# Two down projections of an encoder block: from eight products of block halves to seven

## The chip, the cores and the metric

The kernel runs on one core of a Trainium2 chip. TensorE (PE in the profile, its weight loads PEld) multiplies, VectorE (DVE), ScalarE (ACT) and GpSimd (POOL) do everything else, and SyncE (SP) issues nearly all DMAs. The metric is the device time of one execution in microseconds, the median of three runs: 2277.6 us before (2276.05 to 2281.06).

## The reference, cut to what matters

One layer: a SwiGLU feed-forward network, a token mixer, a second feed-forward network, each inside the same frame of norms. All data are float32; 1024 tokens (S), width 1024 (D), hidden width 2816 (DFF).

```python
def swiglu(h, w_gu, w_down):
    g, u = jnp.split(h @ w_gu, 2, axis=-1)
    return (jax.nn.silu(g) * u) @ w_down
...
def sandwich(x, fn, g_pre, g_post, shift, scale, gate, res_w):
    h = modulate(rmsnorm(x, g_pre), shift, scale)
    y = rmsnorm(fn(h), g_post)
    return x + res_w * gate[:, None, :] * y
...
        mod = (c_act @ w_ada[l] + b_ada[l]).reshape(b, N_SUB, 3, D_MODEL)
...
        x = sandwich(x, ffn1, norm_pre[l, 0], norm_post[l, 0], mod[:, 0, 0], mod[:, 0, 1], mod[:, 0, 2], 0.5)
        x = sandwich(x, mix, norm_pre[l, 1], norm_post[l, 1], mod[:, 1, 0], mod[:, 1, 1], mod[:, 1, 2], 1.0)
        x = sandwich(x, ffn2, norm_pre[l, 2], norm_post[l, 2], mod[:, 2, 0], mod[:, 2, 1], mod[:, 2, 2], 0.5)
```

The change concerns the product with `w_down` (1024 x 2816 by 2816 x 1024), twice, and the nine vectors of `mod`.

## The kernel before

**Numbers.** Every float32 operand is split into a high and a low part (`split`, L135: a cast on ACT, a subtraction on DVE or POOL). A product is three matmuls: high by high, high by low, low by high. A matmul has a 128x128 stationary and a 128x512 moving operand.

**Stages.** First network: an up phase and a down phase; then the recurrent branch, its output (`rec_out_phase`), attention, the merge, the output projection; then the second network, up and down. In the networks PE, DVE, ACT and POOL run in the order in which the code issues (a manual schedule); SP's order, and all engines' order in `rec_out_phase`, come from the scheduler. Each engine works strictly in its order.

**Up phase.** 22 blocks of 128 hidden channels. The first 4 (second network: 3) are plain; the others (`block`, L614) use seven products of halves, Winograd's form of Strassen's scheme, in the order 1, 2, 6, 5, 7, 3, 4. After product i of block fb, `mix(fb + 1, i)` (L581) makes the next block's operand: up to two POOL operations, a cast on ACT, a subtraction on DVE. A block's activations (`act`, 128x1024) go to DRAM (`act_d`).

**Down phase** (L716 to L800). The 22 blocks of the inner dimension are loaded again in seven chunks (`CHUNKS`) of 2 to 4. `down_w` loads and splits one activation or weight block; for each chunk and each of 8 token blocks (`sb`) PE adds up the chunk's products in two PSUM banks, and DVE adds them to `yacc[sb]` (L779). This is the plain product: 22 x 8 x 2 x 3 = 1056 matmuls. The last two chunks are ordered by token halves, so that the first half's epilogue runs beside the second half's matmuls.

**Epilogue.** `put` does the row norm (a square on ACT, an addition and a power on POOL) and multiplies by the gate on POOL; `update` adds the residual on DVE, stores, and starts the next norm (`rstd_of`: ACT, then POOL twice); `norm` scales on DVE; `drain` lets PE transpose four normalized rows for the next stage. `push_last` (L407) ends the kernel.

**Background.** `bgq` is a queue of generators that compute the conditioning vectors; `bg(n)` advances it by n steps. A step of `ada_acc` (L179) loads 512 KB of `w_ada` and adds it to a sum on DVE; `ada_cols` (L193) and `ada_gate` (L259) end with a few matmuls on PE into banks of `trbank`. Before, five such vectors run in the first network (one step a block, one a row step of the down phase), two in `rec_out_phase` (three steps in each of eight iterations, then `bg_flush`).

**Tiles.** Tag `raw` has 3 tiles, `wh` and `wl` 4 each (operands high and low), `t4` 22 big ones, `u` 3. PSUM has 6 banks of tag `ps` and 2 of `tr`.

## Time and profile before

| | us |
|---|---|
| median of 3 runs | 2277.6 |
| profiled execution | 2280.03 |
| its span, first to last instruction | 2278.2 |
| PE busy in the span | 2212.8 |
| first down projection, from 488.0 | 263.2 |
| second down projection, from 2026.8 | 241.2 |

The page below gives the mean over whole slices of the span; the granted clock is nearly full throughout.

```profile
PEclk9999999999999999999999999999999999999999
GB/s 295 103 84 92 110 111 92 111 138 187 189 191 121 77 50 40 66 148 166 111 49 67 25 59 53 157 185 158 97 92 83 83 83 83 82 141 110 93 93 120
```

Each of the 40 columns is 57 us. The down phases are columns 9 to 13 and 36 to 40. Rows of groups read: line, engine, operation, output and inputs, shape, count, then busy time and the mean of one in ns, then the idle time before it and what ended it. The rows on which the argument rests stand with the prediction.

### The profile page before, as it was taken

How to read it: one execution, taken by the hardware profiler on the slowest of the kernel's cores; microseconds unless marked ns; L12 is line 12 of the kernel's file. 1: busy time of each engine (PE TensorE's matmuls, PEld its weight loads, DVE VectorE, ACT ScalarE, POOL GpSimd, SP SyncE). 2: the span in 40 equal slices, each digit the busy share in tenths (PEclk: the TensorE clock that was granted, in tenths of full speed). 3: DMA queues.
4: the chain of work that ended last, by engine and by line, in shares of the span. 5: the costliest groups of instructions: out<-in, count | busy, mean ns of one | idle time of the engine just before them, and what ended most of it. 6: DMA issues, size and time to landing. Idle time of an engine off the chain costs nothing.

```text
span 2278.2 us, 26296 instructions
## 1 busy us (share of the span) xinstructions
PE 2212.8 (97%) x10227; PEld 1837.7 (81%) x10227; DVE 1230.3 (54%) x1740; ACT 945.8 (42%) x1502; POOL 582.3 (26%) x412
## 2 busy tenths in 40 slices
PE   5999999999999999999999999999999999999998
PEld 3877888888778788888898988887788888888886
DVE  6665554535755677643336666546854444433444
ACT  3543333341213587821147777336433333342121
POOL 3432222222225311000021120006432222222224
PEclk9999999999999999999999999999999999999999
DMA  9322332345653211245312011454322222243223
GB/s 295 103 84 92 110 111 92 111 138 187 189 191 121 77 50 40 66 148 166 111 49 67 25 59 53 157 185 158 97 92 83 83 83 83 82 141 110 93 93 120
DMA packets 217748, 250.30 MB, mean 110 GB/s; under 512 B 10864, under 2 KB 172824, under 8 KB 217624
## 3 DMA queue, kind: packets, MB, share of 16 engines
q1 hardware_dynamic: 217512, 248.60, 34.4%
q8 instruction: 80, 1.31, 0.2%
q14 instruction: 44, 0.36, 0.1%
q10 hardware_dynamic: 112, 0.03, 0.0%
HBM read 203.51 MB, written 48.23 MB: 110 GB/s over the span
## 4 chain that ended last, share of the span: by engine, by line
PE 75%; DVE 6%; ACT 4%; DMA 2%; issue 1%; POOL 1%; DVEq 0%; POOLq 0%; ACTq 0%
PE pd L766 17%; PE pj L435 6%; PE pj L433 6%; PE pj L434 6%; PE psX L610 5%; PE psX L612 5%; PE psX L611 5%; PE pj L1064 4%; PE psZ L610 3%; PE psZ L612 3%; PE psZ L611 3%; PE pv L1111 1%; PE psY L610 1%; PE psY L612 1%; PE psY L611 1%
## 5 line engine op out<-in xcount | busy, mean ns | idle before, releaser
L766 PE MATMUL pd<-dh,ah 128*128 128x512 f32 x1440 | 348.9, 393 | 0.0
L766 PEld LDWEIGHTS pd<-dh,ah 128*128 128x128 f32 x1440 | 273.3, 190 | 57.5 <-POOL dh L137 0.5
L434 PE MATMUL pj<-hl,wh 128*128 128x512 f32 x576 | 227.6, 395 | 5.7 <-DVE hl L316 5.7
L435 PE MATMUL pj<-hh,wl 128*128 128x512 f32 x576 | 227.6, 395 | 4.7 <-DVE wl L137 4.1
L433 PE MATMUL pj<-hh,wh 128*128 128x512 f32 x576 | 230.1, 400 | 0.5 <-ACT wh L136 0.5
L779 DVE TENSOR_TENSOR yacc<-yacc,pd 128x512 f32<-128x512 f32 x190 | 121.9, 683 | 193.4 <-PE pd L766 193.2
L601 DVE TENSOR_TENSOR wm<-raw,wm 128x512 fp32r<-128x512 f32 x152 | 109.6, 724 | 160.5 <-ACT wm L600 160.5
L588 POOL TENSOR_TENSOR raw<-wsum,raw 128x512 f32<-128x512 f32 x37 | 48.1, 1299 | 365.7 <-DVE wm L601 360.4
L136 ACT CAST wh<-raw 128x1024 fp32r<-128x1024 f32 (+1 forms) x86 | 86.8, 1011 | 126.5 <-PE pj L434 52.6
L137 POOL TENSOR_TENSOR wl<-raw,wh 128x1024 fp32r<-128x1024 f32 x25 | 61.2, 2456 | 291.9 <-ACT wh L136 247.4
L434 PEld LDWEIGHTS pj<-hl,wh 128*128 128x128 f32 x576 | 109.8, 191 | 29.7 <-DVE hl L316 7.7
L435 PEld LDWEIGHTS pj<-hh,wl 128*128 128x128 f32 x576 | 109.7, 191 | 29.7 <-DVE wl L137 5.7
L433 PEld LDWEIGHTS pj<-hh,wh 128*128 128x128 f32 x576 | 109.8, 191 | 22.9 <-ACT wh L136 0.8
L137 DVE TENSOR_TENSOR wl<-raw,wh 128x1024 fp32r<-128x1024 f32 (+1 forms) x61 | 73.7, 1211 | 84.7 <-ACT wh L136 84.7
L610 PE MATMUL psX<-hh,wm 128*128 128x512 f32 x296 | 115.6, 391 | 2.8 <-ACT mixes L633 2.8
L610 PE MATMUL psX<-hs,wm 128*128 128x512 f32 x296 | 115.3, 389 | 1.6 <-ACT mixes L626 1.6
L612 PE MATMUL psX<-hh,wm 128*128 128x512 f32 x296 | 115.2, 389 | 0.0
L611 PE MATMUL psX<-hl,wm 128*128 128x512 f32 x296 | 115.2, 389 | 0.0
L612 PE MATMUL psX<-hs,wm 128*128 128x512 f32 x296 | 115.2, 389 | 0.0
L611 PE MATMUL psX<-hs,wm 128*128 128x512 f32 x296 | 115.2, 389 | 0.0
L136 ACT CAST dh<-rawd 128x1024 fp32r<-128x1024 f32 x54 | 56.4, 1052 | 138.8 <-DMA rawd<-in_ffn_w_down_dram 105.5
L1064 PE MATMUL pj<-hh,wh 128*128 128x512 f32 x256 | 102.3, 400 | 0.9 <-DVE gate L277 0.9
(303 smaller groups left out, 5283.9 us busy)
## 6 DMA issues: line engine op xcount, KB each, us to landing
rawa<-in_w_ada_dram SPq DMA_DIRECT2D x56, 512.0 KB, 4.3
raw<-in_ffn_w_gu_dram SPq DMA_DIRECT2D x49, 512.0 KB, 4.3
rawd<-act SPq DMA_DIRECT2D x44, 512.0 KB, 3.6
rawd<-in_ffn_w_down_dram SPq DMA_DIRECT2D x44, 512.0 KB, 4.0
raw<-in_w_in_dram SPq DMA_DIRECT2D x44, 512.0 KB, 3.8
sr<-in_ffn_w_gu_dram SPq DMA_DIRECT2D x39, 512.0 KB, 6.4
act<-act SPq DMA_DIRECT2D x37, 512.0 KB, 4.7
rawa<-in_w_ada_dram SPq DMA_DIRECT2D x32, 256.0 KB, 5.6
```

The costliest lines, as they stand in the source:

```text
L136: nc.scalar.copy(hi, raw)
L137: (eng or nc.vector).tensor_tensor(lo, raw, hi.bitcast(F32), op=ALU.subtract)
L433: nc.tensor.matmul(dst, wh[:, kk, :], xhk[:, sl], start=first, stop=False)
L434: nc.tensor.matmul(dst, wh[:, kk, :], xlk[:, sl], start=False, stop=False)
L435: nc.tensor.matmul(dst, wl[:, kk, :], xhk[:, sl], start=False, stop=last)
L601: nc.vector.tensor_tensor(t[:, 1], src, t[:, 0].bitcast(F32), op=ALU.subtract)
L610: nc.tensor.matmul(dst, t[:, 0, kk, :], xh, start=first and kk == 0, stop=False, skip_group_check=True)
L611: nc.tensor.matmul(dst, t[:, 0, kk, :], xl, start=False, stop=False, skip_group_check=True)
L612: nc.tensor.matmul(dst, t[:, 1, kk, :], xh, start=False, stop=last and kk == 3, skip_group_check=True)
L766: nc.tensor.matmul(pd[h], a_[:, tk], w_[:, h * 512 : (h + 1) * 512], start=(i == 0 and j == 0), stop=(i == n - 1 and j == 2),)
L779: nc.vector.tensor_tensor(yacc[sb][:, sl], yacc[sb][:, sl], pd[h], op=ALU.add)
L1064: nc.tensor.matmul(d, a[:, k, :], b[k][:, sl], start=k == 0 and i == 0, stop=k == KB - 1 and i == 2)
```

## The change

The down projection is computed in seven products in place of eight, with the same scheme as the up phase: tokens in two halves, output columns in two halves (`h1`, `h2`), and the inner dimension in 11 pairs of blocks (2j and 2j+1). The seven products run one after the other over all pairs; a *unit* (p, j) is pair j of product p: two loads of 256 KB into one `raw` tile (a half of an activation block, a half of a weight block), one split of 128x1024, and 4 x 3 = 12 matmuls.

- The sums of halves (four POOL operations a pair, for weights and for activations) are made during the up phase by `all_sums`, one step after each product of a block, and stored in DRAM (`act_s`, `down_s`). A pair is loaded one pair ahead. Activations of the Strassen blocks are summed in place, in the tiles that `block` left (`kept`), once both are done; those of plain blocks are loaded again.
- Products 1, 6, 7 and 4 add up in four banks (`chain`), the others in four more; between products ACT copies or DVE adds four banks to `yacc` (`reads`).
- Pairs 4 to 10 of product 4 are fetched between those of product 3 and kept in `t4` tiles. Product 4 then runs pairs 0 to 3 for all four rows of the second token half, and pairs 4 to 10 row by row; the first half's rows are complete with product 3.
- `push_last` reads the last bank directly, without adding it to `yacc` first.
- Background: a load is issued one step before its sum; a step that needs a bank can be held back; two steps a block in the up phase, one a unit in the down phase. Two vectors (`ada_cols(6)`, `ada_cols(7)`) move to `rec_out_phase`, which makes five steps an iteration.

```diff
+    raw_home = ["raw"]
+    BANK = "needs a bank"
     def ada_acc(v, alloc):
         acc = alloc("acc")
         for k in range(KB):
-            raw = wpool.tile([P, 1024], F32, tag="raw", bufs=3, name=nm("rawa"))
+            if raw_home[0] == "t4":
+                raw = t4("rawa")
+            else:
+                raw = wpool.tile([P, 1024], F32, tag="raw", bufs=3, name=nm("rawa"))
             nc.sync.dma_start(raw, w_ada[k * P : (k + 1) * P, v * D : (v + 1) * D])
+            yield None
             if k == 0:
                 nc.vector.tensor_scalar(acc, raw, c_act[:, 0:1], None, op0=ALU.mult)
             else:
                 nc.vector.scalar_tensor_tensor(
                     acc, raw, c_act[:, k : k + 1], acc, op0=ALU.mult, op1=ALU.add
                 )
-            yield None
+        yield None
         yield acc
...
+    at = [None]
+    def bg(n=1, banks=True):
         for _ in range(n):
-            while bgq:
+            while bgq and (banks or at[0] is not BANK):
                 try:
-                    next(bgq[0])
+                    at[0] = next(bgq[0])
                     break
                 except StopIteration:
+                    at[0] = None
                     bgq.pop(0)
...
-            for h, sl in enumerate(halves):
-                junk = tmp[0].tile([P, D], BF16, tag="junk", bufs=2, name=nm("junk"))
-                nc.vector.tensor_tensor(y[:, sl], y[:, sl], pd[h], op=ALU.add)
-                nc.scalar.activation(junk[:, sl], y[:, sl], AF.Square, scale=D ** -0.5, accum_out=sq[h])
-                if h == 0:
-                    nc.vector.tensor_tensor(y[:, sl], y[:, sl], g[:, sl], op=ALU.mult)
+            junk = [tmp[0].tile([P, D], BF16, tag="junk", bufs=2, name=nm("junk")) for _ in range(2)]
+            one = halves[1]
+            nc.scalar.activation(junk[1][:, one], y[:, one], AF.Square, scale=D ** -0.5, accum_out=sq[1])
+            nc.vector.tensor_tensor(y[:, one], y[:, one], g[:, one], op=ALU.mult)
             self.update(sb - 1)
+            one = halves[0]
+            nc.scalar.activation(junk[0][:, one], pd, AF.Square, scale=D ** -0.5, accum_out=sq[0])
+            nc.vector.tensor_tensor(y[:, one], pd, g[:, one], op=ALU.mult)
             r = small("rstd")
...
+            if fb % 2 == 0:
+                first_of[0] = act
+            elif fb - 1 >= direct:
+                kept[fb - 1, fb] = first_of[0], act
...
                     mix(fb + 1, i)
-                    if fb == NF - 1 and i in ORDER[3:]:
-                        down_w(0, ORDER[3:].index(i))
+                    next(jobs, None)
+                    if i in (2, 3):
+                        bg(1)
+                    if fb == NF - 1 and i in ORDER[4:]:
+                        units.fetch(ORDER[4:].index(i) + 1)
+                ready[0] = fb
                 block(fb, after)
...
+        PAIRS = NF // 2
+        STREAM = (1, 2, 6, 5, 7, 3, 4)
+        act_of = {1: (act_d, 0, 0), 2: (act_d, 1, 0), 4: (act_d, 1, 1), 6: (act_s, 0, 0),
+                  7: (act_s, 0, 1), 3: (act_s, 1, 0), 5: (act_s, 1, 1)}
+        down_of = {1: (w_down, 0, 0), 2: (w_down, 1, 0), 3: (w_down, 1, 1), 5: (down_s, 0, 0),
+                   7: (down_s, 0, 1), 4: (down_s, 1, 0), 6: (down_s, 1, 1)}
+        ready = [0]
...
+        kept = {}
+        def pair_load(j, weights):
+            if not weights and (2 * j, 2 * j + 1) in kept:
+                return kept.pop((2 * j, 2 * j + 1))
+            src = w_down if weights else act_d
+            top, bot = t4("top"), t4("bot")
+            nc.sync.dma_start(top, rows(src, 2 * j))
+            nc.sync.dma_start(bot, rows(src, 2 * j + 1))
+            return top, bot
+        def pair_sums(j, weights, top, bot):
+            dst = down_s if weights else act_s
+            t1, t2, b1, b2 = top[:, h1], top[:, h2], bot[:, h1], bot[:, h2]
+            add, sub_ = ALU.add, ALU.subtract
+            if weights:
+                steps = ((t1, t2, t1, sub_), (t2, b2, t2, sub_), (b2, b2, t1, sub_), (b1, b1, b2, sub_))
             else:
+                steps = ((b2, t2, b2, add), (t2, t1, t2, sub_), (t1, b2, t1, sub_), (b1, b1, t1, sub_))
+            for o, p, q, op in steps:
+                nc.gpsimd.tensor_tensor(o, p, q, op=op)
+                yield
+            yield
+            nc.sync.dma_start(rows(dst, 2 * j), top)
+            nc.sync.dma_start(rows(dst, 2 * j + 1), bot)
...
+            reload_ = [j for j in range(PAIRS) if 2 * j < direct]
+            todo = [(j, True) for j in range(PAIRS)]
+            for n, j in enumerate(reload_):
+                todo.insert(2 * n + 2, (j, False))
+            later = [j for j in range(PAIRS) if j not in reload_]
+            nxt = pair_load(*todo[0])
+            yield
+            yield
+            while todo or later:
+                if later and ready[0] > 2 * later[0] + 1:
+                    j = later.pop(0)
+                    yield from pair_sums(j, False, *pair_load(j, False))
+                elif todo:
+                    now, tiles = todo.pop(0), nxt
+                    if todo:
+                        nxt = pair_load(*todo[0])
+                    yield from pair_sums(*now, *tiles)
+                else:
+                    yield
+        jobs = all_sums()
...
+        class Units:
+            def __init__(self):
+                self.order = [(p, j) for p in STREAM for j in range(PAIRS)]
+                first, last = self.order[:-2 * PAIRS], self.order[-PAIRS:]
+                third = self.order[-2 * PAIRS : -PAIRS]
+                self.order = first
+                for j in range(PAIRS):
+                    self.order.append(third[j])
+                    if j + KEPT_FROM < PAIRS:
+                        self.order.append(last[j + KEPT_FROM])
+                self.order += last[:KEPT_FROM]
+                self.n, self.got = 0, {}
+            def fetch(self, n):
+                while self.n < min(n, len(self.order)):
+                    p, j = self.order[self.n]
+                    raw = wpool.tile([P, 2, 512], F32, tag="raw", bufs=3, name=nm("rawd"))
+                    for o, (t, k, half) in enumerate((act_of[p], down_of[p])):
+                        nc.sync.dma_start(raw[:, o], rows(t, 2 * j + k)[:, (h1, h2)[half]])
+                    if p == STREAM[-1] and j >= KEPT_FROM:
+                        hi, lo = t4("dh", F32R, (P, 2, 512)), t4("dl", F32R, (P, 2, 512))
+                    else:
+                        hi, lo = (wpool.tile([P, 2, 512], F32R, tag=t, bufs=4, name=nm("dh")) for t in ("wh", "wl"))
+                    split(raw, hi, lo, nc.gpsimd if p in (2, 5, 7) and j % 3 == 2 else nc.vector)
+                    self.got[p, j] = hi, lo
+                    self.n += 1
+            def take(self, p, j, ahead):
+                self.fetch(self.order.index((p, j)) + 1 + ahead)
+                return self.got.pop((p, j))
...
+            def mm(dst, i, ops, first, last):
+                hi, lo = ops
+                tk = slice(i * P, (i + 1) * P)
+                for n, (a_, w_) in enumerate(((hi, hi), (hi, lo), (lo, hi))):
+                    nc.tensor.matmul(
+                        dst, a_[:, 0, tk], w_[:, 1, :], start=first and n == 0, stop=last and n == 2,
+                        skip_group_check=True,
+                    )
...
+            reads = {
+                1: ((copy, 0, h1),), 2: ((add, 0, h1),), 6: ((copy, 0, h2),),
+                5: ((copy, half, h2), (add, 0, h2)), 7: ((add, half, h2),), 3: ((add, 0, h2),),
             }
...
+            chain = [bank("px"), bank("px"), trbank("px"), trbank("px")]
+            tr_home[0], raw_home[0] = "ps", "t4"
+            for p in STREAM[:-1]:
+                own = p in (1, 6, 7)
+                dst = chain if own else [bank("pv") for _ in range(4)]
+                for j in range(PAIRS):
+                    ops = units.take(p, j, 3)
+                    for i in range(half):
+                        mm(dst[i], i, ops, j == 0 and p not in (6, 7), j == PAIRS - 1)
+                    next(jobs, None)
+                    bg(1, own)
+                if p == 2:
+                    for _ in jobs:
+                        pass
+                if p == 7:
                     bg_flush()
...
+                for op, sb0, sl in reads[p]:
+                    for i in range(half):
+                        op(sb0 + i, sl, dst[i])
...
+            p = STREAM[-1]
+            for j in range(KEPT_FROM):
+                ops = units.take(p, j, 3)
+                for i in range(half):
+                    mm(chain[i], i, ops, False, False)
+                if j == 0:
+                    units.fetch(len(units.order))
+                epi.put(j, yacc[j])
+                if j > 0:
+                    epi.update(j - 1)
+                if j > 1:
+                    epi.norm(j - 2)
+            last_steps = {4: ((3,), (2, 3), 2), 5: ((4,), (), 4), 6: ((5,), (4,), 2), 7: ((6,), (5,), KB)}
+            for i in range(half):
+                sb = half + i
+                for j in range(KEPT_FROM, PAIRS):
+                    mm(chain[i], i, units.got[p, j], False, j == PAIRS - 1)
+                if tail and i == half - 1:
+                    epi.push_last(sb, yacc[sb], chain[i])
+                    break
+                copy(sb, h1, chain[i])
+                epi.put(sb, yacc[sb])
+                updates, norms, n_out = last_steps[sb]
+                for n in updates:
+                    epi.update(n)
+                for n in norms:
+                    epi.norm(n)
+                if ahead:
+                    ahead.fetch(i + 1)
+                    epi.drain(n_out, on_act=(1, 1))
+                epi.fetch(sb + 1)
...
-            bg(3)
+            bg(5)
...
-        bgq.extend([mixer_constants(), ada_cols(6), ada_cols(7), ada_gate(0, 0.5), ada_cols(3), ada_cols(4)])
+        bgq.extend([mixer_constants(), ada_gate(0, 0.5), ada_cols(3), ada_cols(4)])
...
-        bgq.extend([ada_gate(1, 1.0), ada_gate(2, 0.5)])
+        bgq.extend([ada_cols(6), ada_cols(7), ada_gate(1, 1.0), ada_gate(2, 0.5)])
```

106 lines of the change are left out of this document (27 added, 79 removed).

## The prediction

> **What bounds the kernel now.** I read the page's busy table first, then its chain, then the windows around the two down projections, then what TensorE waited for there.
>
> ```profile
> span 2278.2 us, 26296 instructions
> PE 2212.8 (97%) x10227; PEld 1837.7 (81%) x10227; DVE 1230.3 (54%) x1740; ACT 945.8 (42%) x1502; POOL 582.3 (26%) x412
> PE 75%; DVE 6%; ACT 4%; DMA 2%; issue 1%; POOL 1%; DVEq 0%; POOLq 0%; ACTq 0%
> 488.00:751.20 263.20, 257.32 (x1141) 212.29 (x1140) 153.39 (x165) 76.60 (x99) 86.21 (x53) 0.97 0.53 170
> 2027.00:2268.20 241.20, 239.69 (x1056) 197.67 (x1054) 99.00 (x123) 58.59 (x72) 78.33 (x42) 1.00 0.34 112
> 316.00:335.00 19.00, 19.00 (x86) 15.72 (x85) 9.75 (x14) 6.85 (x12) 5.57 (x4) 1.00 0.34 110
> PE pc L200 <- DVE acc L187: 3.8, 2, 2.2
> PE pd L766 <- POOL dl L137: 1.3, 1, 1.3
> ```
>
> PE is busy for 97% of the span, and three quarters of the chain is PE. In a window row come the length, then the busy time of PE, PEld, DVE, ACT and POOL, then the granted clock, the DMA share and GB/s. The second down projection (2027 to 2268.2) is 1056 matmuls in 239.69 us: **0.227 us a matmul**, with nothing between them. The first (488 to 751.2) has the same 1056 and lasts 263.2 us, because gate vectors (pc, pg) and transposes are done in between, PE waits for two of them (the 3.8 us), and the clock falls to 0.97. An up-projection block (316 to 335) leaves DVE half idle and POOL at 5.57 of 19 us. So a matmul taken away is time taken away, if the other engines then still feed PE.
>
> **The change, part by part.**
>
> *Matmuls.* A product has 11 pairs x 4 token blocks x 3 = 132; seven make 924 a projection in place of 1056. 2 x 132 x 0.227 = **-59.9**. The same shape is used (128x128 stationary, 512 moving), so I keep the rate.
>
> *Entry.* Each projection now begins with one 1.3 us wait for a POOL subtraction (the first is the last row above). The new first unit is split on DVE, and its load can start in the block before: **-2.7** for both; between -2.7 and +3, should the first load come late.
>
> *Gate vectors in the first projection.*
>
> ```profile
> 620.50:625.80 5.30, 3.12 (x17) 3.12 (x17) 3.32 (x3) 0.86 (x1) 1.05 (x1) 0.75 0.62 201
> 625.80:632.50 6.70, 6.70 (x22) 5.39 (x22) 0.80 (x3) 0.19 (x1) 0.00 (x0) 0.69 0.26 97
> ```
>
> Here PE waits for a DVE sum, does its 16 narrow matmuls, and then runs at clock 0.69: 22 matmuls in 6.7 us where 22 x 0.227 = 5.0 would do, so 1.7 are lost beside the wait. In the new order loads run a step ahead of their sums and the steps lie in the up phase. The matmuls stay; the waits (3.8) and twice the 1.7 may go: 7.2 at most, 0 at least. I take **-6**, nearer the rows.
>
> *Feeding the stream.* A unit is 12 matmuls, 12 x 0.227 = 2.72 us of PE.
>
> ```profile
> rawd<-act SPq DMA_DIRECT2D x44, 512.0 KB, 3.6
> raw<-in_w_att_o_dram SPq DMA_DIRECT2D x8, 256.0 KB, 2.9
> sr<-in_ffn_w_gu_dram SPq DMA_DIRECT2D x39, 512.0 KB, 6.4
> L136 ACT CAST dh<-rawd 128x1024 fp32r<-128x1024 f32 x54 | 56.4, 1052 | 138.8 <-DMA rawd<-in_ffn_w_down_dram 105.5 <-PE pd L766 19.8 <-DMA rawd<-act 13.5
> L137 DVE TENSOR_TENSOR dl<-rawd,dh 128x1024 fp32r<-128x1024 f32 x10 | 12.2, 1221 | 13.0 <-ACT dh L136 13.0
> L137 POOL TENSOR_TENSOR dl<-rawd,dh 128x1024 fp32r<-128x1024 f32 x22 | 57.9, 2633 | 173.3 <-ACT dh L136 172.0 <-PE pd L766 1.3
> L779 DVE TENSOR_TENSOR yacc<-yacc,pd 128x512 f32<-128x512 f32 x190 | 121.9, 683 | 193.4 <-PE pd L766 193.2
> ```
>
> A raw tile is held from issue to split: two 256 KB loads (between the 2.9 of a single one and the 3.6 of 512 KB, I take 3.6) + 1.05 + 1.22, about 5.9 us, and there are three: a unit every 2.0 us, faster than 2.72. Units split on POOL hold one for 7.3, still 2.4. So six products stream without waits; the four reads between products (4 x 0.68 on DVE) are covered by three units split ahead (8.2 us).
>
> **Product 3 is different**: with each of its first seven units goes one of product 4, so 14 units are due in 7 x 2.72 = 19.0 us, 1.36 each, and the raw tiles give 2.0. At its start three units are split and three loaded. The seventh comes at 9.8 (2.7 of reads on DVE, 1.2 for the split that frees a tile, a turn of 5.9), and the fifteenth, with which PE goes on at 19.0, at 9.8 + 8 x 2.0 = 25.8: a wait of 6.8, or 4 if the loads land in 2.9. I take **+6 a projection, +12**; 0 if the tiles turn in 4 us, 10 if they take 7. SP's queue holds only these loads then.
>
> *End of the first projection.* Today:
>
> ```profile
> 699.78 0.22 POOL L305 TENSOR_SCALAR rstd<-rstd 128x1 f32<-128x1 f32 x1 [7.41 <-ACT junk L304]
> 721.72 1.01 POOL L306 TENSOR_TENSOR rstd<-rstd,nhalf 128x1 f32<-128x1 f32 x1
> 722.76 0.75 DVE L382 TENSOR_SCALAR yacc<-xr,rstd 128x1024 f32<-128x1024 f32 x1 [0.46 <-POOL rstd L306]
> 725.82 1.04 PE L335 MATMUL pt<-ident,yacc 128*128 128x128 f32 x8
> L365 POOL TENSOR_TENSOR yacc<-yacc,gate 128x1024 f32<-128x1024 f32 x14 | 33.6, 2400 | 0.0
> ```
>
> POOL does four row epilogues and four second norms from 699.8 to 722.7, some 21 us of work and two short waits; then DVE scales row 3 and PE transposes at 725.8, late enough that it never waits. New: rows 0 to 3 all end with product 3 (call it T). PE has 48 + 21 = 69 matmuls (15.7 us) until row 4, and then, in its order, the transposes of rows 0 to 3. But `put(4)` stands before `update(3)`, so POOL does row 4's scale, add and power (3.2) before row 3's second norm: 2.6 to start (a DVE read, an ACT cast that stands first, a square) + 21.2 + 3.2 = T+27.0, and 0.75 for DVE. PE waits from T+15.7 to T+27.8: **+12**. Row 5's matmuls stand behind it. I add **+2** for a slow clock after it, from the 1.7 above. Bounds: 0 (if something reorders PE) to 17.
>
> The Trainium skill, "TensorE: Matmul & The Clock Gate", Part 1, says that an idle window of about 3.4 us halves the clock and that about as long a busy one restores it; an estimate by it is 1.7 us, as this trace lost after a wait of 2.2 and narrow matmuls.
>
> *End of the recurrent output.* Four vectors now pass here in place of two: 46 steps, five after each of eight blocks, so six are left for the flush.
>
> ```profile
> 1056.64 0.75 DVE L185 TENSOR_SCALAR acc<-rawa,c_act 128x1024 f32<-128x1024 f32 x1
> 1082.56 1.29 DVE L187 SCALAR_TENSOR_TENSOR acc<-rawa,c_act,acc 128x1024 f32<-128x1024 f32 x1 [4.95 <-DMA rawa<-in_w_ada_dram]
> 1117.81 1.36 DVE L1006 SCALAR_TENSOR_TENSOR tg<-tg,pj 128x512 f32<-128x512 f32 x2 [8.07 <-PE pj L435]
> 1131.20 0.50 PE L1064 MATMUL pj<-hh,wh 128*128 128x512 f32 x1 [0.92 <-DVE gate L277]
> ```
>
> Attention's first matmul already waits for the last gate add (0.92). A sum of eight loads took 27 us here (1056.6 to 1083.8), 1.9 each at best by the turn of raw tiles (4.3 + 1.28, over three). The last sum can start only when the vector before it lets its tile go, near 1120, so it may end at 1136 to 1147, and PE would wait 4 to 14. The scheduler orders this phase, so 0 is possible; I take **+5**.
>
> *Sums in the up phase.*
>
> ```profile
> L588 POOL TENSOR_TENSOR raw<-raw 128x512 f32<-128x512 f32 x37 | 47.9, 1294 | 74.1 <-DVE wm L601 73.9
> act<-act SPq DMA_DIRECT2D x37, 512.0 KB, 4.7
> L601 DVE TENSOR_TENSOR wm<-wsum,wm 128x512 fp32r<-128x512 f32 x1 | 1.6, 1589 | 2.0 <-ACT wm L600 2.0
> L601 DVE TENSOR_TENSOR wm<-sr,wm 128x512 fp32r<-128x512 f32 x2 | 1.4, 692 | 0.0
> ```
>
> 22 pairs x 4 POOL operations of 1.29 are 114 us a projection, 5.6 operations a block: POOL goes from 5.6 to about 13 of 19 us. Traffic rises by 35 MB over 18 or 19 blocks (11 each for weights in and out, 2 for direct activations in, 11 out), from 110 to about 210 GB/s, more than the 170 of the first down projection's row. What stands behind a waiting sum on POOL is the mix for the next block, and ACT's cast and copies behind that. An activation sum overwrites a tile whose store (4.7 us) starts as the block begins; three or four of nine pairs a projection come in that first step. POOL is then free at about 8 us and its mix is done by 10, before the copy at 10.9 on which PE depends. The tag of 22 big tiles is nearly full (12 sums of the hidden state, two or three activations, four of two pairs, one or two weights, one for mixes), so a pair load now and then waits on SP for a store of 4.7 us, and the weight loads behind it; these and the doubled gate vector loads are due a block (19 us) later. **+3**, bounds 0 and 30.
>
> *Tail.*
>
> ```profile
> 2267.65 0.39 PE L766 MATMUL pd<-dh,dl 128*128 128x512 f32 x1
> 2273.71 1.41 DVE L426 SCALAR_TENSOR_TENSOR xr<-yacc,rstd,xr 128x512 f32<-128x512 f32 x2 [0.44 <-POOL rstd L423]
> ```
>
> From PE's end (2268.0) to 2278.2 are 10.2 us. New: row 6 ends 4.8 before PE does; its copy, square and POOL work end 0.9 after PE, then 1.28 + 0.68 + 1.1 + 1.41 on DVE and POOL and the 3.1 that today follow the last DVE write: 8.6. **-1.6**.
>
> *Sum:* -59.9 - 2.7 - 6 + 12 + 14 + 5 + 3 - 1.6 = **-36.2**. The profiled execution took 2280.03 (span 2278.2): 2243.8. It stands 2.4 above the median, so 2241.4, said as **2241**.
>
> **Rivals.**
>
> 1. *PE stays fed.* Raw tiles turn faster than 5.9 and the scheduler hides the flush, while POOL's order still costs little: only the terms with a minus sign count, -70.2, so 2207. For it: DVE, ACT and POOL stand at 54, 42 and 26%. Against it: POOL's order at T, which nothing shortens. With that wait alone it is 2221.
>
> 2. *The sums hold up the up phase.* Each of 18 in-place sums waits for a store slower than 4.7 us in doubled traffic, 1.5 us reaching PE: +27 in place of +3, so 2265. The row of 1589 beside 692 shows a DVE subtraction that POOL delays by 0.9; seven a block are 6.3, and DVE's 9.75 becomes 16 of 19, not a bound. The Trainium skill, "SBUF — State Buffer", Who interferes with whom, says that a DVE operation with two SBUF inputs and a POOL operation that reads SBUF exclude each other for a whole instruction; the trace agrees with those two rows.
>
> 3. *Slower: the stream starves.* If a raw tile's turn passes 3 x 2.72 = 8.2 us, every unit costs PE more than 2.72, and product 3's 12 us are part of that. The other 48 us of gain are used up when 154 units lose 0.31 each: a turn of 9.1, that is, loads landing in 6.8 us. The 6.4 row shows that crowded moments come near it; the 3.6 row, from the down projections themselves, speaks against it. At 7.0 us the turn is 9.3 and the loss 57: 2241 - 12 + 57 = 2286.
>
> **How the numbers follow.** Forecast 0.57 (own range 2226 to 2256), rival 1 0.20, rival 2 0.12, near no change 0.03, rival 3 0.08. A measurement of this kernel can tell about 0.2% (4.6 us) from no change. Range: down to rival 1 with most of its gains, up past rival 2: 2208 to 2268. Faster 0.89, same 0.03, slower 0.08.
>
> **What would show it.** The down projections' matmuls count 924 each at 0.227 us. Right: PE idle in product 3 before matmuls that wait for DVE's split; a wait of about 12 us before the transposes of yacc, ended by DVE's scaling; attention's first matmul after 1131 by the old clock, waiting for the gate add; up blocks of 19.05 us. Wrong: blocks longer than 19.3, waits spread through all products, or transposes without a wait.

## The result: slower, and the profile after

The changed kernel takes 2297.4 us (median of 4 runs, 2293.6 to 2303.3) where the kernel before takes 2277.3 us (4 runs, 2276.1 to 2281.1). The ratio is 1.0088, with an interval of 1.0063 to 1.0113: **slower by about 20 us**, where 36 us less were forecast. The profiled execution took 2296.16 us, with a span of 2294.4.

First the page of the changed kernel: its span, the busy time of the engines, and the chain of work that ended last.

```profile
span 2294.4 us, 26847 instructions
PE 2169.8 (95%) x9963; PEld 1792.0 (78%) x9963; DVE 1317.9 (57%) x1676; ACT 1016.9 (44%) x1567; POOL 798.5 (35%) x558
PE 67%; DVE 12%; DMA 7%; ACT 6%; POOL 4%; issue 3%; SPq 1%; DVEq 0%; ACTq 0%; POOLq 0%
```

PE does what the change promises, 264 matmuls fewer (10227 to 9963), but its busy time falls by 43.0 us where 264 x 0.227 would be 59.9. Matmuls that run longer at a lower clock count as busy, and the mean granted clock of the run is 0.982 where it was 0.992; the last kernel below has the same 9963 matmuls and 2155.5 us, 57.3 less than before. PE's share of the span falls from 97% to 95%, and its share of the chain from 75% to 67%. POOL's busy time rises from 582.3 to 798.5 us. So the work went away, and waits and a slower clock came in its place.

Next the windows of the changed kernel: one stretch of the first network's up phase, an up block later in it, the first and the second down projection (columns as in the prediction's windows).

```profile
196.00:215.00 19.00, 9.95 (x36) 7.74 (x35) 15.79 (x31) 3.46 (x7) 10.12 (x8) 0.73 0.19 63
300.00:319.00 19.00, 19.00 (x85) 15.71 (x84) 14.41 (x15) 7.47 (x14) 16.00 (x11) 1.00 0.89 308
519.50:768.50 249.00, 225.49 (x976) 183.12 (x975) 115.75 (x107) 112.47 (x132) 60.66 (x45) 0.95 0.62 198
2061.70:2281.00 219.30, 212.59 (x925) 172.76 (x923) 101.31 (x89) 94.50 (x106) 53.13 (x31) 1.00 0.63 202
```

The last row comes near the forecast: 924 matmuls (and one at the edge) in 219.3 us, where the old second projection took 241.2 (21.9 less, and 25.3 less were forecast). In the second row an up block is still full, although POOL now works 16.0 of 19 us where it worked 5.57. The first row is the surprise: PE busy for 9.95 of 19 us, at a granted clock of 0.73.

What PE waited for in the changed kernel, by stretch: the first network's up phase (four rows), its down projection (four), the recurrent output (one), the second down projection (two). Rows under 1 us are left out. Columns: total us, times, the longest.

```profile
PE psX L630 <- DVE pp L640: 10.4, 3, 9.0
PE psX L630 <- ACT mixes L653: 7.4, 3, 3.6
PE psZ L630 <- ACT pp L657: 4.5, 3, 2.9
PE psX L630 <- ACT mixes L646: 1.4, 1, 1.4
PE pt L352 <- DVE yacc L399: 13.9, 3, 5.1
PE pc L214 <- DVE acc L200: 3.5, 1, 3.5
PE pv L856 <- DVE dh L143: 3.0, 4, 0.8
PE pv L856 <- ACT dh L142: 2.0, 3, 0.9
PE pg L289 <- ACT acch L142: 13.2, 1, 13.2
PE pv L856 <- DVE dh L143: 3.5, 5, 0.8
PE pv L856 <- ACT dh L142: 1.8, 3, 0.7
```

The first up phase of the kernel before, with one background step a block and no pair sums, has two rows, 4.4 us in all:

```profile
PE psX L610 <- ACT mixes L633: 2.8, 2, 1.9
PE psX L610 <- ACT mixes L626: 1.6, 1, 1.6
```

The table cuts the run into stages. A stage begins with the first matmul of its kind, read from the rows of those tiles, but for three: the recurrent output begins with the last matmul of the recurrence's gate, and the two ends of the second down projection are the starts of the last Strassen and the last down matmul. The forecast column sorts the terms of the prediction's sum by stage.

| stage | before, us | after, us | change | forecast |
|---|---|---|---|---|
| first up phase | 350.3 | 381.7 | **+31.4** | +1.5 |
| first down projection, to the recurrence | 308.3 | 291.9 | -16.4 | -17.3 |
| recurrence | 157.5 | 157.6 | +0.1 | 0 |
| recurrent output, to attention's first score | 199.3 | 220.6 | **+21.3** | +5 |
| attention to the end of the second up phase | 873.4 | 871.8 | -1.6 | +1.5 |
| second down projection | 241.1 | 219.3 | -21.8 | -25.3 |
| from the last matmul to the end | 10.6 | 13.7 | **+3.1** | -1.6 |

The three bold rows hold the miss: 29.9 + 16.3 + 4.7 = 50.9 of the 52.4 us between a forecast of -36.2 and a span that grew by 16.2.

The first of them can be read in the timeline of the changed kernel, at its longest wait. Columns: start, duration, engine, line, operation; in brackets the idle time before it and what ended it.

```profile
197.29 1.30 POOL L782 TENSOR_TENSOR act<-act,act 128x512 f32<-128x512 f32 x1
197.40 1.21 DVE L961 TENSOR_TENSOR sp_s<-sp_s 128x8 f32<-128x8 f32 x1
198.65 0.17 DVE L962 TENSOR_SCALAR sp_pl<-sp_s 128x8 f32<-128x8 f32 x1
198.67 1.30 POOL L782 TENSOR_TENSOR act<-act 128x512 f32<-128x512 f32 x1
198.85 1.14 DVE L964 TENSOR_TENSOR sp_pl<-sp_pl,sp_s 128x8 f32<-128x8 f32 x1
...
209.13 0.68 DVE L640 TENSOR_TENSOR pp<-psX,pp 128x512 f32<-128x512 f32 x1
...
209.87 0.80 PE L630 MATMUL psX<-hs,wm 128*128 128x512 f32 x1 [9.05 <-DVE pp L640]
```

The 128x8 operations are the mixer's constants, one background step. Each that starts beside a POOL operation ends with it, after 1.1 to 1.2 us; one that starts between two of them takes 0.17. The whole chain holds VectorE from 194.7 to 207.9; in the kernel before, without pair sums, the same chain took 6.4 us in an up block (202.0 to 208.3). VectorE's queue runs in order: two subtractions of mixes follow the chain, and the read of PSUM on which PE depends (L640) starts only at 209.13.

A second wait shows the same thing without the constants:

```profile
284.66 1.42 POOL L782 TENSOR_TENSOR act<-act,act 128x512 f32<-128x512 f32 x1 [2.82 <-issue]
284.85 2.31 DVE L200 SCALAR_TENSOR_TENSOR acc<-rawa,c_act,acc 128x1024 f32<-128x1024 f32 x1
286.17 2.14 POOL L782 TENSOR_TENSOR act<-act 128x512 f32<-128x512 f32 x1
288.26 1.26 POOL L608 TENSOR_TENSOR raw<-wsum,raw 128x512 f32<-128x512 f32 x1
289.55 0.62 ACT L620 CAST wm<-raw 128x512 fp32r<-128x512 f32 x1 [4.86 <-POOL raw L608]
290.08 0.58 ACT L657 COPY pp<-psZ 128x512 f32<-128x512 f32 x1
290.71 0.50 PE L630 MATMUL psZ<-hh,wm 128*128 128x512 f32 x1 [2.93 <-ACT pp L657]
```

A gate vector's sum (L200, 1.28 us where nothing is beside it) takes 2.31 us beside a pair sum, and the next pair sum takes 2.14 instead of 1.30. POOL's mix for the next block (L608) stands behind them, ACT's cast behind the mix, ACT's copy behind the cast, and PE behind the copy.

Not all of the 23.7 us are of this kind. A third wait has a late load behind it:

```profile
405.89 0.62 ACT L620 CAST wm<-raw 128x512 fp32r<-128x512 f32 x1 [6.83 <-DMA raw<-in_ffn_w_gu_dram]
410.12 0.80 PE L630 MATMUL psX<-hh,wm 128*128 128x512 f32 x1 [3.57 <-ACT mixes L653]
```

SP issued this load of the next block's weights at 397.4, and it is there at 405.9, 8.5 us later; the median of such loads is 5.2, and in this stretch the DMA engines are full (share 1.02, 337 GB/s). Behind that cast stand, one after the other, VectorE's subtraction and addition and ACT's activation, cast and copy, for which PE waits. A fourth wait (3.48 us, at 154.0) stands behind five small loads of the constants that ACT issues itself, from 149.8 to 153.3, again with the DMA engines full; with the sums taken out (below) the wait in that place is 1.84 us. So some 7 of the 23.7 us go through loads.

### The profile page after: what moved, and what is told of

Its sections match the earlier page's. It is cut to its first block, busy times and chain, and to the rows that moved or that the text cites. A ratio compares the mean times of both kernels' runs of the same rounds, so it can differ in the third digit from the quotient of the medians.

```text
span 2294.4 us, 26847 instructions
## 1 busy us (share of the span) xinstructions
PE 2169.8 (95%) x9963; PEld 1792.0 (78%) x9963; DVE 1317.9 (57%) x1676; ACT 1016.9 (44%) x1567; POOL 798.5 (35%) x558
## 3 DMA queue, kind: packets, MB, share of 16 engines
q8 instruction: 78, 1.28, 0.2%
## 4 chain that ended last, share of the span: by engine, by line
PE 67%; DVE 12%; DMA 7%; ACT 6%; POOL 4%; issue 3%; SPq 1%; DVEq 0%; ACTq 0%; POOLq 0%
PE pj L450 6%; PE pj L452 6%; PE pj L451 6%; PE px L856 6%; PE pv L856 5%; PE pj L1194 5%; PE psX L630 4%; PE psX L631 4%; PE psX L632 4%; PE psZ L630 2%; PE psZ L632 2%; PE psZ L631 2%; DVE wm L621 2%; PE pv L1241 1%; DMA rawd<-in_ffn_w_down_dram 1%
## 5 line engine op out<-in xcount | busy, mean ns | idle before, releaser
L143 DVE TENSOR_TENSOR dh<-rawd,dh 128x1024 fp32r<-128x1024 f32 x122 | 153.9, 1264 | 191.9 <-ACT dh L142 191.4
L142 ACT CAST dh<-rawd 128x1024 fp32r<-128x1024 f32 x154 | 161.9, 1053 | 221.9 <-DMA rawd<-in_ffn_w_down_dram 70.2
L450 PE MATMUL pj<-hh,wh 128*128 128x512 f32 x576 | 229.9, 399 | 0.5 <-ACT wh L142 0.5
L856 PE MATMUL px<-dh,dh 128*128 128x512 f32 x592 | 183.7, 392 | 1.5 <-DVE dh L143 1.5
L856 PE MATMUL pv<-dh,dh 128*128 128x512 f32 x528 | 165.2, 394 | 6.5 <-DVE dh L143 6.5
L856 PE MATMUL px<-dh 128*128 128x512 f32 x352 | 139.5, 396 | 1.0 <-ACT dh L142 1.0
L452 PEld LDWEIGHTS pj<-hh,wl 128*128 128x128 f32 x576 | 109.4, 190 | 29.9 <-DVE wl L143 5.7
L856 PEld LDWEIGHTS px<-dh,dh 128*128 128x128 f32 x592 | 111.7, 189 | 25.6 <-DVE dh L143 2.4
L630 PE MATMUL psX<-hs,wm 128*128 128x512 f32 x296 | 117.3, 396 | 12.1 <-DVE pp L640 10.4
L630 PE MATMUL psX<-hh,wm 128*128 128x512 f32 x296 | 117.8, 398 | 7.4 <-ACT mixes L653 7.4
L856 PEld LDWEIGHTS pv<-dh,dh 128*128 128x128 f32 x528 | 99.1, 189 | 30.4 <-DVE dh L143 10.0
```

What stands on the lines that cost most here:

```text
L142: nc.scalar.copy(hi, raw)
L143: (eng or nc.vector).tensor_tensor(lo, raw, hi.bitcast(F32), op=ALU.subtract)
L450: nc.tensor.matmul(dst, wh[:, kk, :], xhk[:, sl], start=first, stop=False)
L452: nc.tensor.matmul(dst, wl[:, kk, :], xhk[:, sl], start=False, stop=last)
L630: nc.tensor.matmul(dst, t[:, 0, kk, :], xh, start=first and kk == 0, stop=False, skip_group_check=True)
L856: nc.tensor.matmul(dst, a_[:, 0, tk], w_[:, 1, :], start=first and n == 0, stop=last and n == 2, skip_group_check=True,)
```

## Experiments

The theory after the traces: (1) in the first up phase it is not the pair sums that cost, but background steps and pair sums **together**; (2) the recurrent output pays for two more vectors; (3) the last rows are bound by POOL's epilogue. The rivals: the sums alone, their stores or their traffic; two steps inside a block by their place alone; a chance order of the scheduler. Each of the first eight kernels ran once, so the stages of their profiles are compared with the changed kernel's; stages that an edit doesn't touch differ by 1 to 3 us.

### The first up phase: take out the steps, then the sums

```
-                    if i in (2, 3):
-                        bg(1)
```

> The background steps of the first up phase (constants of the mixer, sums of gate vectors, their narrow matmuls) are taken out of its blocks; all 39 of them now go with the units of the first down projection. The pair sums on GpSimd stay where they are. In the changed kernel TensorE waits 23.7 us between 100 and 520 us, against nearly none before, and 2.9 us in the second network's up phase, which has the same pair sums and no such steps. Theory A (the steps beside the sums hold up the mixes): the wait of 23.7 falls below 5 us, the first down projection begins about 29 us earlier (519.5 to about 490), of which 7.6 are matmuls that move with the steps and come back in the down projection; the whole run is 12 to 20 us shorter, about 2280. Theory B (the sums themselves, or their stores, hold up the up phase): the wait stays above 15 us, and the run is within 8 us of 2297.

What PE waited for in the first up phase of this kernel:

```profile
PE psX L630 <- ACT mixes L646: 1.5, 1, 1.5
PE psX L630 <- ACT mixes L653: 0.8, 1, 0.8
```

The waits fall from 23.7 to 2.3 us, with all sums and their loads and stores in place; of the traffic only 18 of the steps' own 24 loads left, and the phase moves 194 GB/s where it moved 202. POOL now waits five times, 27.3 us in all, for a store before an in-place sum, and PE waits for none of it; ACT, which had waited 21.4 us for late weight loads, no longer waits for any. The span is 2263.6 us, 30.8 less, and the run took 2265.4 us where the kernel before took 2273.3 beside it. That is more than the 12 to 20 expected: the up phase lost 36.0 us (21.4 of waits, 3.1 of matmuls that left it, and the rest by the clock, whose mean over the phase is 1.00 where it was 0.97), and the down projection got back only 6.5. The constants, now in the down projection and beside an idle POOL, run at their own speed (timeline of this kernel, one of them):

```profile
505.62 0.17 DVE L958 TENSOR_TENSOR sp_s<-sp_ee,sp_den 128x8 f32<-128x8 f32 x1
```

The counterpart keeps the steps and takes the pair sums out of the first up phase; they are done after product 1, which makes the whole run long (2407 us) and only the up phase readable.

```
-                    next(jobs, None)
+                    if sub:
+                        next(jobs, None)
...
-            elif fb - 1 >= direct:
+            elif fb - 1 >= direct and sub:
...
-                if p == 2:
+                if p == (2 if sub else 1):
```

> The counterpart of the first run: in the first network's up phase the pair sums are taken out of the blocks (they are done in the down projection's first product, where TensorE will have to wait for them), and the background steps stay in the blocks. Only the length of the up phase counts here, 381.7 us in the changed kernel, 345.7 us without the background steps. Theory A (it takes both, steps and sums, to hold up the mixes): waits of TensorE in the up phase below 4 us, and its length 345.7 plus the 6 to 8 us of the vectors' matmuls, 350 to 356. Theory B (two steps inside a block hold up the mixes by their place alone): waits above 12 us and a length above 365. The whole run is expected above 2297, by 20 us and more, for the sums stand late.

What PE waited for in the up phase of this kernel:

```profile
PE psX L630 <- DVE pp L640: 4.1, 1, 4.1
PE psX L630 <- ACT mixes L653: 1.8, 1, 1.8
PE psX L630 <- ACT mixes L646: 1.4, 1, 1.4
```

That is 7.3 us, more than the 4 expected, and the phase is 356.8 us long, 0.8 above the expected end. So steps without sums leave 7.3 us of waits, sums without steps 2.3, and both 23.7: the two together cost at least 23.7 - 7.3 - 2.3 = 14.1 us of waiting more than the parts (a kernel with neither was not run, so the 7.3 and 2.3 may hold a common share). The gate vectors' sums show it one by one (groups by line in the up phase, first the changed kernel, then this one; busy us and mean ns):

```profile
L200 DVE SCALAR_TENSOR_TENSOR acc<-rawa,c_act,acc 128x1024 f32<-128x1024 f32 x19 | 29.4, 1547 | 0.0
```

```profile
L200 DVE SCALAR_TENSOR_TENSOR acc<-rawa,c_act,acc 128x1024 f32<-128x1024 f32 x19 | 24.3, 1279 | 0.0
```

The Trainium skill, "SBUF — State Buffer", Who interferes with whom, says that a VectorE instruction with two SBUF inputs, or one in a mode that uses both ports, and a GpSimd instruction that reads SBUF block each other for the whole of an instruction; the 0.17 that became 1.1 to 1.2 and the 1.28 that became 2.31 agree. Whether the late weight loads come from the three `raw` tiles, which the steps' loads share with them, or from the DMA engines being full, no run separates.

Third, the constants alone are moved out of the up blocks:

```
-        bgq.extend([mixer_constants(), ada_gate(0, 0.5), ada_cols(3), ada_cols(4)])
+        bgq.extend([ada_gate(0, 0.5), ada_cols(3), ada_cols(4), mixer_constants()])
```

> The constants of the mixer stand last in the first network's background queue, no longer first, so that their short operations (about 26 on VectorE on 128x8 tiles) fall into the first down projection and not into an up block. The other background steps stay in the up blocks, two a block. In the changed kernel these operations take 1.1 to 1.26 us each beside GpSimd's sums and 0.17 us elsewhere, and TensorE waits 9.05 us behind them at 209.9; the other waits of the up phase come to 14.7 us. Theory A (any background step beside the sums costs, the constants most in one place): the up phase (first Strassen product to first product of the down projection, 381.7 us) shrinks by 9 to 13 us and keeps waits of 8 to 15 us. Theory B (the constants are all of it): it shrinks by 20 us or more. Theory C (the steps are innocent): it shrinks by less than 4 us.

The wait of 9.05 us is gone, but the up phase is only 4.3 us shorter (377.4), and 18.5 us of waits remain: the gate sums moved up into the constants' place, and other waits came (mixes L653 8.9 us in six waits, where there were three of 7.4; the longest, 3.75 at 237.5, stands behind a late weight load again). Neither number is as expected under theory A, and 4.3 is close to theory C's bound of 4. The run refutes theory B, that the constants are all of it; that the steps are not innocent is shown by the first run, not by this one.

### The recurrent output

```
-        bgq.extend([mixer_constants(), ada_gate(0, 0.5), ada_cols(3), ada_cols(4)])
+        bgq.extend([mixer_constants(), ada_gate(0, 0.5), ada_cols(3), ada_cols(4), ada_cols(6), ada_cols(7)])
...
-            bg(5)
+            bg(3)
...
-        bgq.extend([ada_cols(6), ada_cols(7), ada_gate(1, 1.0), ada_gate(2, 0.5)])
+        bgq.extend([ada_gate(1, 1.0), ada_gate(2, 0.5)])
```

> The two gate vectors that were moved from the first network to the recurrent output go back (as the last of the first network's queue), and the recurrent output again does three steps a block. Theory A (the recurrent output is longer by 21.3 us because its last vector's sum ends late and its narrow matmuls run beside an idle TensorE at a granted clock of 0.80): pgate to attention's first score matmul shrinks by 17 to 22 us, and the first network grows by 2 to 8 us for the matmuls and loads that return; run about 2280. Theory B (the recurrent output is longer for another reason, for example the order that the scheduler finds): it shrinks by less than 8 us; run within 6 us of 2297.

PE's waits in the recurrent output of this kernel:

```profile
PE pg L290 <- DVE acch L143: 2.0, 1, 2.0
PE pg L289 <- ACT acch L142: 1.0, 1, 1.0
```

The wait of 13.2 us for the last vector's sum is down to 1.0, with 2.0 for its low part. The stage takes 205.2 us, 15.4 less, and the first network's down stage 5.8 more; the span is 2281.4. That is short of theory A's 17 to 22 and far from theory B's 8: A's cause holds, its size doesn't quite. In the changed kernel the window around that wait (1150 to 1165 us) has PE busy for 3.0 of 15 us at a clock of 0.59.

### Product 3

```
-                    raw = wpool.tile([P, 2, 512], F32, tag="raw", bufs=3, name=nm("rawd"))
+                    if p in STREAM[-2:]:
+                        raw = hpool.tile([P, 2, 512], F32, tag="h", bufs=16, name=nm("rawh"))
+                    else:
+                        raw = wpool.tile([P, 2, 512], F32, tag="raw", bufs=3, name=nm("rawd"))
```

> The raw tiles of the last two products come from the 16 slots that the hidden state leaves free in a down projection, not from the three raw tiles. Nothing else is changed. Theory A (in product 3 TensorE waits 6 to 7 us a projection because three raw tiles turn in 5.9 us each): the waits in both third products fall below 2 us each; the run is 8 to 12 us shorter, about 2287. Theory B (the loads, two of 256 KB a unit at twice the rate of a unit, do not come faster, or the splits on VectorE are the limit): each stays above 4 us; the run is within 4 us of 2297.

What PE waited for in the second down projection of this kernel:

```profile
PE px L859 <- DVE dh L143: 0.4, 1, 0.4
PE pv L859 <- DVE dh L143: 0.3, 1, 0.3
```

The second projection's waits, 6.8 us with two in its first product, are 0.7, and those of the first one's product 3 are gone too. The span is 2277.9, 16.5 less (8 to 12 were expected), of which 5.3 and 8.3 in the two down stages and 1.8 in the tail, which is 12.0 to 12.1 in two later kernels with these tiles as well; the 1.2 in the first up phase is not the edit's. So it was the turn of three raw tiles, and neither the loads' rate nor the splits.

### The transposes and the tail

The first try reorders the epilogue: POOL's part of row 4 goes behind row 3's norm, and the transposes behind rows 6 and 7.

```
-                epi.put(sb, yacc[sb])
                 updates, norms, n_out = last_steps[sb]
+                if i or not ahead:
+                    epi.put(sb, yacc[sb])
...
+                if ahead and i == 0:
+                    epi.put(sb, yacc[sb])
...
-            last_steps = {4: ((3,), (2, 3), 2), 5: ((4,), (), 4), 6: ((5,), (4,), 2), 7: ((6,), (5,), KB)}
+            last_steps = {4: ((3,), (2, 3), 0), 5: ((4,), (), 0), 6: ((5,), (4,), 4), 7: ((6,), (5,), KB)}
```

> In the first network only: the scale and add of row 4 and its power come after the update of row 3 and the norms of rows 2 and 3 on GpSimd, and the transposes of rows 0 to 3 move from behind rows 4, 5 and 6 to behind row 6 (four) and row 7 (the rest). Theory A (TensorE waits 13.9 us for the transposes because GpSimd does row 4 ahead of row 3's norm, and because the transposes stand too early in TensorE's order): that wait falls to under 3 us; the run is 8 to 14 us shorter, or less if the eight rows then end late behind the last product (a new wait at the beginning of the recurrent projection). Theory B (the wait is moved, not removed): the first projection's end to the recurrent gate's first matmul stays within 4 us.

PE's waits for the transposes at the end of the first down projection in this kernel:

```profile
PE pt L352 <- ACT h L341: 4.2, 2, 4.0
PE pt L352 <- DVE yacc L399: 3.1, 2, 2.0
```

Theory B: the stage took 291.5 instead of 291.9 us. The transposes still wait (4.2 and 3.1 us), and the recurrent projection waits behind them (1.8 us for DVE's hl). In this kernel POOL is busy from 719.8, the end of product 3, to 761.4 almost without a gap; this order doesn't make it shorter.

The tail was tried by itself, with more room for the residual's rows:

```
-                self.xr[sb] = tu("xr")
+                if self.make:
+                    self.xr[sb] = tu("xr")
+                else:
+                    self.xr[sb] = hpool.tile([P, 1024], F32, tag="h", bufs=16, name=nm("xrh"))
```

> In the last down projection the rows of the residual come into slots that the hidden state leaves free, not into the three that are shared with the outgoing rows. Theory A (the tail, from TensorE's last matmul to the end, is 13.35 us and not 10.2 because the last rows' residual is loaded late, when an outgoing row's store has landed): the tail falls to 8.5 to 10 us, the run to about 2293. Theory B (the tail is set by the row's own chain of operations): it stays above 12 us.

From the last down matmul to the end it is 13.0 us, against 13.7: theory B. Its timeline on VectorE shows why:

```profile
2274.89 1.28 DVE L391 SCALAR_TENSOR_TENSOR xrh<-yacc,rstd,xrh 128x1024 f32<-128x1024 f32 x1 [3.13 <-POOL yacc L385]
2279.30 1.28 DVE L391 SCALAR_TENSOR_TENSOR xrh<-yacc,rstd,xrh 128x1024 f32<-128x1024 f32 x1 [3.12 <-POOL yacc L385]
```

The rows come 4.41 us apart, each released by POOL's multiplication: POOL does 4.41 us a row without a break from the end of product 3. It is again the four rows that finish at once, so one edit should serve both places. It runs product 3 first and 7 before 4, so that rows 0 to 3 are complete a product earlier:

```
-        STREAM = (1, 2, 6, 5, 7, 3, 4)
+        STREAM = (3, 1, 2, 6, 5, 7, 4)
...
-                    split(raw, hi, lo, nc.gpsimd if p in (2, 5, 7) and j % 3 == 2 else nc.vector)
+                    split(raw, hi, lo, nc.gpsimd if p in (2, 5) and j % 3 == 2 else nc.vector)
...
-                1: ((copy, 0, h1),), 2: ((add, 0, h1),), 6: ((copy, 0, h2),),
-                5: ((copy, half, h2), (add, 0, h2)), 7: ((add, half, h2),), 3: ((add, 0, h2),),
+                1: ((copy, 0, h1),), 2: ((add, 0, h1),), 6: ((add, 0, h2),),
+                5: ((copy, half, h2), (add, 0, h2)), 7: ((add, half, h2),), 3: ((copy, 0, h2),),
...
+            def early(j):
+                if j in (1, 3, 5, 7):
+                    epi.put(j // 2, yacc[j // 2])
+                if j in (3, 5, 7, 9):
+                    epi.update(j // 2 - 1)
+                if j in (6, 8, 10):
+                    epi.norm(j // 2 - 3)
...
```

> The order of the seven products is changed from 1, 2, 6, 5, 7, 3, 4 to 3, 1, 2, 6, 5, 7, 4 in both networks, so that rows 0 to 3 are complete before product 7 and not before product 4; their scale, add, update and norm go with product 7's units, their transposes with the last units of product 4. GpSimd then splits only in products 2 and 5. Theory A (the wait of 13.9 us for the transposes is GpSimd's epilogue of rows 0 to 3, which starts too late): that wait falls below 3 us, and the time from the first down projection to the first gate matmul of the recurrence (291.9 us) shrinks by 10 to 17 us. Theory B (GpSimd's or VectorE's work is only moved into the product in which two products are split at once, which then waits more): the waits in product 7 exceed 10 us a projection, and the stage shrinks by less than 6 us. The second network's down projection should change by less than 3 us by theory A. Run: about 2283 by A, 2291 or more by B.

PE's waits from product 7 of the first projection on:

```profile
PE px L859 <- DVE yacc L872: 6.1, 1, 6.1
PE px L859 <- ACT dh L142: 4.6, 2, 2.9
PE px L859 <- DVE dh L143: 3.2, 4, 1.2
```

No transpose waits any more, which agrees with the reading of the 13.9 us: POOL's epilogue of rows 0 to 3 begins too late. (The edit also frees POOL of product 7's splits and moves the transposes; the parts weren't tried apart.) And the tail falls to 8.1 us. But 13.9 us of new waits stand in these rows: product 7 now shares VectorE and ACT with the epilogue, and product 4 writes the banks that product 7 has just filled (6.1 us until VectorE has read them). The stage is 5.4 us shorter where theory A wanted 10 to 17, and the second projection 8.0 longer: in time it went theory B's way. The span is 2287.9.

### Together

The next two kernels join the edits that worked (no steps in the first up phase, the two vectors back, raw tiles from the free slots), the second with a milder form of the other order.

> Three of the earlier edits together: no background steps in the first up phase, the two gate vectors back in the first network, raw tiles of products 3 and 4 from the hidden state's slots. Alone they gave -30.8, -13.0 and -16.5 us of span against the changed kernel's 2294.4. If they are independent: 2294.4 - 60.3 = 2234 us of span, about 0.98 of the time before. If they share something (61 background steps now fall on the 66 units of one down projection, so that their flush before product 3 gets longer): 2240 to 2252. Should it be above 2260, the single runs were partly drift of the chip.

2261.7 us, a ratio of 0.993 to the kernel before (0.9909 to 0.9951): faster, but with a span of 2262.0 and not the 2234 of independent parts. PE's waits in the first down projection:

```profile
PE pc L214 <- DVE acc L200: 21.1, 2, 10.9
```

Sixty-one background steps don't fit into the units, and the flush before product 3 waits for two vectors in a row, 10.9 and 10.2 us, with nothing beside them. The span is also above the 2260 from which the single runs were to be put down to drift. But 20.5 of the 28 us by which it misses stand in one stage, the first down projection (319.4 us; the three edits one by one add up to 298.9), and the other stages are within 3 us of the single runs: drift may be in these few us, not in the 20.5.

> The three edits and the order 3, 1, 2, 6, 5, 7, 4, in which rows 0 to 3 are complete a product earlier. In the run of that order alone the wait for the transposes (13.9 us) was gone and the tail was 8.1 in place of 13.7 us, but product 4 then waited 6.1 and 5.1 us for VectorE's additions of product 7, behind splits of units of product 4 and a norm that stood ahead of them in its queue; here those stand behind the additions, and the raw tiles have 16 slots. Theory A: 12 to 20 us less than the kernel with three edits, about 2218 of span. Theory B (the additions between products 7 and 4, on the same banks, cost what the transposes gave): within 5 us of the kernel with three edits.

2265.3 us, 0.9948 (0.993 to 0.9967). The wait for the transposes is gone and the tail is 8.2 us, but the vectors now have to be done before product 7, eleven units sooner; one more of them falls into the flush, and the same wait is 35.4 us. The time is theory B's, within 5 us of the kernel with three edits, but not by B's cause: no wait for the additions of product 7 is left.

So the vectors were spread by the rate of their loads: a step that needs a bank no longer holds up the next vector's loads, one column vector goes with the first network, one column and one gate vector with the recurrent output, and the last network's gate vector with that network's own units.

```
-            while bgq and (banks or at[0] is not BANK):
+            pos = 0
+            while pos < min(2, len(bgq)):
+                if not banks and at.get(bgq[pos]) is BANK:
+                    pos += 1
+                    continue
...
+        bgq.extend([mixer_constants(), ada_gate(0, 0.5), ada_cols(3), ada_cols(4), ada_cols(6)])
...
+        bgq.extend([ada_cols(7), ada_gate(1, 1.0)])
...
-        load_gate(2)
+        bgq.append(ada_gate(2, 0.5))
```

> As the kernel with three edits and the other order, but the six vectors are spread by the rate of their loads: five of the first network's background jobs (constants, one gate, three of the columns) stay in its down projection, one step a unit, and where the first of two jobs waits for a bank the second one loads on; one column vector and one gate vector are left in the recurrent output (three steps a block), and the last network's gate vector goes with the units of its own down projection. In the two runs before, the flush of the vectors cost waits of 21 and 35 us (10.9 to 12.8 a vector). Theory A (those waits were loads of 4 MB a vector in a row, at the rate of the queue, which nothing hid): they fall below 5 us, and the span comes to 2262 - 21 - 14 (transposes) - 6 (tail) - about 3 more of slow clock, about 2218 to 2225. Theory B (the down projection can't take the vectors' loads beside its own at all): waits for the splits appear in all products and the span stays above 2250.

> The same without the other order of the products (1, 2, 6, 5, 7, 3, 4 as in the changed kernel). It tells what the order is worth once the vectors are spread. Theory A: the wait for the transposes stays at 13 to 16 us and the tail at 13 us, the span is 16 to 22 us above the kernel with the other order, 2236 to 2245. Theory B (the order gains nothing): within 6 us of it.

| kernel | us (4 runs) | ratio to before | interval |
|---|---|---|---|
| changed | 2297.4 | 1.0088 | 1.0063 to 1.0113 |
| spread, order of the change | 2244.4 | 0.9854 | 0.9839 to 0.9869 |
| spread, product 3 first | **2235.1** | **0.9813** | 0.9797 to 0.9829 |

The page of the last one:

```profile
span 2232.5 us, 26771 instructions
PE 2155.5 (97%) x9963; PEld 1786.7 (80%) x9963; DVE 1317.2 (59%) x1682; ACT 1013.6 (45%) x1567; POOL 784.6 (35%) x552
```

PE is back at 97%, and the sums on POOL (784.6 us busy) are still all there. The waits for vectors in the first down projection are 5.8 us in place of 39.4 (pc and pg). The span missed its expected 2218 to 2225 by 7.5 us. The order was worth 6.9 us of span and not 16 to 22: it saved 10.5 up to the recurrence, but the second down projection with its tail took 230.8 us against 227.0; product 7 waits there for VectorE's splits (6.9 us). An order changed in the first network alone wasn't tried.

## Why the prediction was wrong

**Right.** *Matmuls*: 924 a projection at the same rate; in the second projection 924 x 0.227 = 209.7 of the 219.3 us. *Product 3*: +6 a projection forecast; the waits of pv were 5.0 and 5.3, by the mechanism named, the three raw tiles' turn. *End of the first projection*: +12 forecast, 13.9 measured in three waits, by POOL's late norms and PE's fixed order.

**Partly luck.** The sum for the two down projections was -17.3 and -25.3 against -16.4 and -21.8. In the first, 7.3 us of the saving are narrow matmuls that moved to other stages, which the forecast, summing over all places, had at nothing. They stand in for the gate vectors' term (-6): of the 3.8 us of waits that it took away, 3.5 are still there (pc).

**Wrong: "Sums in the up phase", +3.** This step failed, and it is the largest miss: +31.4 in the first up phase where its half of the term was +1.5. The prediction had the in-place sums waiting for stores, and POOL, the mix and ACT's copy late behind them. The path from POOL to PE is that of the second wait shown above; the stores are not the cause, since 27.3 us of waiting for them cost PE nothing once the steps were gone. It priced the sums as if the blocks stayed as they were, and in another step it moved the gate vectors into the same blocks and counted only what that saves (-6). What the two do to each other was priced nowhere, but for a clause that the vectors' loads are due a block later. The runs: sums alone 2.3 us of waits, steps alone 7.3, both 23.7, and 30.8 us of span by the steps' removal. Of the 23.7, some 12 (the waits of 9.05 and 2.93) are VectorE and POOL holding each other up, and some 7 go through loads; the rest, waits of at most 1.4, wasn't followed back. Rival 2 had the right row (a subtraction of 1589 beside 692 ns) and the right rule beside it, but spent it on VectorE's busy share, "16 of 19, not a bound". The share wasn't the point: VectorE and POOL run in order, and behind the stretched operations stood one that PE needed at once. The second up phase, with the same sums and no steps, has no such wait.

**Wrong: the flush of the recurrent output, +5.** The mechanism was right, the size not: bounds of 4 to 14 us stood for the wait, and it was 13.2, near the far end. To that come the slow clock behind it and the narrow matmuls that moved there (two rows of 16, 1.84 us each). Giving the two vectors back returned 15.4 us in this stage.

**Wrong: the tail, -1.6.** It was +3.1. The prediction followed only the last rows from their own end. Rows 0 to 3 all finish with product 3 in the second network as well, which the prediction worked out for the first network alone; POOL is then behind until the end, 4.41 us a row.

**Small.** The entry term (-2.7) came to nothing: the wait at the first matmul is gone, but two splits of the first product are late by 1.1 us in the first projection and by 1.5 in the second. It and the stages between can hardly be told from the 1 to 3 us by which single profiles of one stage differ here. Rival 3, the only slower one, gave 2286 but by starving loads, which no run showed: with 16 raw tiles the stream hardly waited. The forecast's 36 us were nearly there to be had in the change's own order of products, 33.4 once the vectors are spread and the raw tiles are more; with product 3 first it is 42.7.

## What to carry to other kernels

When a change moves two kinds of work into the same stretch, price the pair: list what VectorE and GpSimd would run side by side there, and look for the operation that PE waits for behind them, however low the busy shares are. Look too for the loads that the two kinds of work put into one queue and one set of tiles. Where an engine finishes several rows at one instant, follow its queue until it is empty, at each place of the kernel where that happens. A list of small jobs spread over loop units is only hidden while both its loads and its steps fit; what is left for a flush stands in the open at the full time of its loads.

## What was not expected of the hardware

An operation of 0.17 us on a 128x8 tile cost as much as the POOL operation beside it, 1.1 to 1.2 us, so that a chain of some two dozen took 13 us (194.7 to 207.9 in the changed kernel's timeline; 4.4, from 505.2 to 509.5, beside an idle POOL in the kernel without steps). Two operations could also stretch each other in turn: 2.31 us for 1.28 on VectorE, then 2.14 for 1.30 on POOL. The traffic, which the prediction feared, did less than feared, but not nothing: an up block at 308 GB/s was as full as one at 110, yet one weight load took 8.5 us, and PE lost 3.57 us by it.
